# Two pairs of transformer blocks on one core: a new order at the start of the second block, the keys' rotation on GpSimd, four modulation loads moved, tables in larger steps

## The chip, the cores and the metric

The kernel runs on one core of a Trainium2 chip. A core has TensorE (PE, with its weight loads as PEld), VectorE (DVE), ScalarE (ACT), GpSimd (POOL) and the sync engine (SP), which here only issues transfers. Each engine takes its own instructions strictly in their order; semaphores tie the engines together. The metric is the device time of one execution in microseconds (us).

## The reference, cut to what matters

There are 256 tokens of width 1024. Two layers of a first block come first, and then two layers of a second block; every layer has weights of its own, all in float32.

```python
for l in range(2):                                   # first_block
    sh1, sc1, g1, sh2, sc2, g2 = split(silu(c) @ w_ada[l] + b_ada[l], 6)
    h = rms_norm(x, norm1_g[l]) * (1 + sc1) + sh1
    q, k, v, iq, ik, iw, z, xbc, dt_raw, ga, gm = split(h @ w_in[l])
    q = apply_rope(rms_norm(q), cos, sin); k = apply_rope(rms_norm(k), cos, sin)   # 16 heads of 64
    o_attn = dsa_attention(q, k, v, iq, ik, iw, 64) @ w_attn_o[l]   # each query keeps its 64 best keys
    o_ssm = ...                                      # a state space scan of z, xbc, dt
    x = x + g1 * ((sigmoid(ga) * o_attn + sigmoid(gm) * o_ssm) @ w_out[l])
    u = causal_dwconv((rms_norm(x, norm2_g[l]) * (1 + sc2) + sh2) @ w_up[l])
    x = x + g2 * ((silu(gate) * val) @ w_down[l])    # val, gate = split(u)
for l in range(2):                                   # second_block
    cq, ckv, kpe, gq, gk, gv, glr, gr, su, gates = split_in(rms_norm(x, norm1_g[l]) @ w_in[l])
    o_a = mla_mixer(cq, ckv, kpe, ...)               # 8 heads: norm, rope, softmax attention
    bc = cumsum(log_sigmoid(glr @ w_gate + b_gate) / 16)   # GLA, in chunks of 64 tokens
    o_b = gla(gq * exp(bc), gk * exp(-bc), gk * exp(b_last - bc), gv, gr)
    y = gelu(s5(su) + d * su)                        # a scan over the tokens, 512 channels
    o_c = y * sigmoid(y @ w_glu + b_glu)
    g = sigmoid(gates + gate_b).reshape(..., 3, 1024)
    merged = g[0]*(o_a @ w_br_mla) + g[1]*(o_b @ w_br_gla) + g[2]*(o_c @ w_br_s5)
    x = x + merged @ w_out[l]
    x = x + square(relu(rms_norm(x, norm2_g[l]) @ w_ff1[l])) @ w_ff2[l]
```

## The kernel before

**Weights.** All weights come from memory as one stream of pieces of 128x1024 floats, `raw`, issued on SP (L460). `make` splits each piece in two numbers of lower precision: ACT copies it into `whi` (L463), and DVE takes `raw - whi` into `wlo` (L464). There are 5 buffers of raw, 4 of whi, 3 of wlo. The activations are split alike (`hh` and `hl`, `oah` and `oal`, `yhlh` and `yhll`). A product is then three matmuls: high by high (L499), low by high (L500), high by low (L501) in `lin_t`, whose result has 128 columns of weights on the partitions and 256 tokens, and L522 to L524 in `lin_n`, whose result has the tokens on the partitions. One `lin_t` over a depth of 1024 is 24 matmuls and one piece of weights; over a depth of 512 it is 12 matmuls. Results of `lin_t` and `lin_n` lie in four PSUM buffers `pmm`; other results of PE lie in buffers `px`.

**Order.** The program is written in Python; a scheduler sets the order of each engine's instructions from the order in which the program is written, from priorities, and from the dependencies. Side work is written as generators, which `paced` advances by a few steps between two products. `tc.issue_after(x)` orders what is in its scope behind instruction x.

**First block.** The modulation (`w_ada`) comes as 48 loads a layer (`ada`, 512 KB each, in the same stream), which DVE multiplies and adds up (L718), ACT gathers (L732) and PE sums (L733). ADA_A names the columns that lie in the first stage of a layer, ADA_DOWN those of layer 1 that lie in the last stage (w_down) of layer 0. The rotation (rope, `rope_n`, L805 to L811) of q and k takes six operations of 128x512 for each of two halves of the tokens; `kr` and `qr` are the rotated keys and queries, which PE then turns (L689). The index scores and the choice of 64 keys (L986 to L989) make a `bias`, which DVE adds to the scores (L832), ACT takes exp (L838) and scales (L841), and PE turns the result (L850). `s5_prep` makes tables for the second block (L661 to L669: phases, sine and cosine) in steps beside w_up and w_down; PDN is its steps for each column of w_down.

**Second block.** `block2` makes the MLA heads' `mq`, `mk`, `mv`, then `la`, the logarithm of GLA's gate: log1p by DVE in a chain of dependent operations (`log1pexp_neg`, L676 to L683, then L1599, L1600) and the running sum `ge` (L1604, eight scans). Ten exponentials on ACT (L1606 to L1611) read it. `gv` is a `lin_n` with 512 columns, two buffers of pmm, moved out by ACT (L1617). Then comes a loop over 24 gate products n (`lin_t`, L1693 the tanh that moves each out); after n = 3 `linear_qk` is written. In each turn of the loop `paced(chain, CHAIN)` does CHAIN steps of `chains`, 35 in all: the MLA heads' norm and rope on DVE (L1650, six of L805 to L811, L1655, then four transposes L689; eight such sets), GLA, and the attention. Every third turn does a step of `s5_run`: for each quarter q of the channels L1464, L1468 to L1481, then L1489 and L1493 on PE, L1496 on ACT, a transfer to memory (L1497, on ACT's queue) and back (L1500, on SP's queue) into `yt`, and L1504. After the loop come `branch(1)` and `branch(0)` (8 products of depth 512 each), gelu (L1717) and split (L554, L555) of the S5 result, four products `s5_w_glu_2`, which give `oc` (L1725, L1726) and its split `och`, `ocl` (L551, L552), and `branch(2)`.

`slot` gives buffers of 4 KB for each partition from a pool of NSLOT; `crow` holds a row form of silu(c) for some of the ada loads.

## Time and profile before

| what | value |
|---|---|
| median of 3 runs | 2246.64 us (2245.1 to 2252.94) |
| the profiled execution | 2245.79 us |
| its span, first to last instruction | 2243.8 us |
| mean granted TensorE clock | 0.98 |
| busy share of PE, DVE, ACT, POOL | 95%, 77%, 60%, 5% |

The profile is of one execution. [...] The difference between the execution's time and its span, 2.0 us, lies around the span.

### The profile page before, as it was taken

What the parts mean: (1) busy time and instruction counts of PE and PEld (TensorE: products, weight loads), DVE (VectorE), ACT (ScalarE), POOL (GpSimd) and SP (SyncE); (2) the same over time, 40 slices, a digit from 0 to 9 for tenths busy, and PEclk for the clock granted to TensorE, in tenths of its full rate; (3) what the DMA queues carried; (4) which work ended last, traced back from release to release, by engine and by line L of the source; (5) the groups of instructions that cost most, each with busy time, mean ns of one, the idle gap of its engine ahead of it and who ended that gap; (6) DMA issues with size and microseconds to landing.
All of it is one profiled execution on the core that took longest, in us unless ns stands there. A gap on an engine that the chain in (4) does not pass through costs nothing. (4 is left out here: it accounts for less than half of the span.)

```text
span 2243.8 us, 44306 instructions
## 1 busy us (share of the span) xinstructions
PE 2140.3 (95%) x17296; PEld 2024.6 (90%) x17296; DVE 1732.6 (77%) x3349; ACT 1336.3 (60%) x2461; POOL 116.5 (5%) x122
## 2 busy tenths in 40 slices
PE   7998999999998997999989999899999997999999
PEld 6888789998997886889989998899999997999999
DVE  4888888889887888788889787677875577678753
ACT  4546866466646557775576566585664464755643
POOL 0210011000000210011000001000000010000000
PEclk9999999999999998999999999899999998999999
DMA  8755344856685653444746666444555564444553
GB/s 324 246 206 197 138 166 152 296 198 208 224 286 188 225 190 132 167 162 164 263 159 199 200 242 225 135 157 158 177 190 182 174 218 135 150 160 162 195 180 123
DMA packets 143457, 429.09 MB, mean 191 GB/s; under 512 B 34864, under 2 KB 40976, under 8 KB 143248
## 3 DMA queue, kind: packets, MB, share of 16 engines
q1 hardware_dynamic: 136496, 422.24, 55.4%
q10 hardware_dynamic: 6752, 4.02, 0.6%
q8 instruction: 136, 2.23, 0.4%
q14 instruction: 73, 0.60, 0.1%
HBM read 413.98 MB, written 12.22 MB: 190 GB/s over the span
## 5 line engine op out<-in xcount | busy, mean ns | idle before, releaser
L463 ACT ACTIVATE whi<-raw 128x1024 fp32r<-128x1024 f32 x639 | 674.8, 1059 | 592.4 <-PE pmm L500 356.1
L464 DVE TENSOR_TENSOR wlo<-raw,whi 128x1024 fp32r<-128x1024 f32 x639 | 781.8, 1225 | 295.0 <-PE pmm L501 161.8
L499 PE MATMUL pmm<-hh,whi 128*128 128x256 f32 x2432 | 698.3, 288 | 31.8 <-ACT fh L554 14.9
L501 PE MATMUL pmm<-hh,wlo 128*128 128x256 f32 x2432 | 693.0, 286 | 4.1 <-DVE wlo L464 4.1
L500 PE MATMUL pmm<-hl,whi 128*128 128x256 f32 x2432 | 694.2, 286 | 0.0
L499 PEld LDWEIGHTS pmm<-hh,whi 128*128 128x128 f32 x2432 | 470.0, 194 | 40.8 <-ACT fh L554 15.2
L501 PEld LDWEIGHTS pmm<-hh,wlo 128*128 128x128 f32 x2432 | 469.3, 194 | 9.2 <-DVE wlo L464 4.9
L500 PEld LDWEIGHTS pmm<-hl,whi 128*128 128x128 f32 x2432 | 470.5, 194 | 4.4 <-issue 3.8
L499 PE MATMUL pmm<-fh,whi 128*128 128x256 f32 x864 | 244.6, 284 | 2.1 <-ACT whi L463 2.0
L500 PE MATMUL pmm<-fl,whi 128*128 128x256 f32 x864 | 244.2, 283 | 0.0
L501 PE MATMUL pmm<-fh,wlo 128*128 128x256 f32 x864 | 243.5, 283 | 0.0
L499 PEld LDWEIGHTS pmm<-fh,whi 128*128 128x128 f32 x864 | 165.7, 192 | 2.8 <-ACT whi L463 2.5
L500 PEld LDWEIGHTS pmm<-fl,whi 128*128 128x128 f32 x864 | 165.7, 192 | 0.1
L501 PEld LDWEIGHTS pmm<-fh,wlo 128*128 128x128 f32 x864 | 165.3, 192 | 0.2
L560 POOL TENSOR_TENSOR rr<-rv,mhalf 128x2 f32<-128x2 f32 (+3 forms) x26 | 55.5, 2136 | 1173.3 <-DVE rv L565 1173.3
L523 PE MATMUL pmm<-wlo,hh 128*128 128x512 f32 x256 | 102.6, 403 | 0.0
L522 PE MATMUL pmm<-whi,hh 128*128 128x512 f32 x256 | 95.9, 403 | 1.7 <-ACT hh L548 1.5
L524 PE MATMUL pmm<-whi,hl 128*128 128x512 f32 x256 | 97.3, 398 | 0.0
L718 DVE SCALAR_TENSOR_TENSOR raw<-raw,crow 128x1024 f32<-128x1024 f32 x44 | 53.8, 1223 | 25.6 <-DMA raw<-in_ada 25.6
L499 PE MATMUL pmm<-yh,whi 128*128 128x256 f32 x256 | 71.6, 283 | 0.1
L500 PE MATMUL pmm<-yl,whi 128*128 128x256 f32 x256 | 71.5, 283 | 0.0
L501 PE MATMUL pmm<-yh,wlo 128*128 128x256 f32 x256 | 71.5, 284 | 0.0
(560 smaller groups left out, 4242.0 us busy)
## 6 DMA issues: line engine op xcount, KB each, us to landing
raw<-in_w SPq DMA_DIRECT2D x639, 512.0 KB, 4.1
raw<-in_ada SPq DMA_DIRECT2D x96, 512.0 KB, 4.5
csb<-csd SPq DMA_DIRECT2D x16, 512.0 KB, 5.7
phd<-phases SPq DMA_DIRECT2D x8, 512.0 KB, 2.9
phasel<-phd SPq DMA_DIRECT2D x8, 512.0 KB, 3.9
dpd<-dp SPq DMA_DIRECT2D x4, 512.0 KB, 3.7
gl<-gd SPq DMA_DIRECT2D x32, 64.0 KB, 3.4
bl<-in_s5b SPq DMA_DIRECT2D x4, 512.0 KB, 5.6
```

The costliest lines, as they stand in the source:

```text
L463: S.activation(hi, raw, AF.Copy)
L464: st["lo"] = V.tensor_tensor(lo, raw, hi, OP.subtract).ins
L499: PE.matmul(ps[:m, :n], wh, src.hi(kt), start=q == 0, stop=False)
L500: PE.matmul(ps[:m, :n], wh, src.lo(kt), start=False, stop=False)
L501: st["mm"] = PE.matmul(ps[:m, :n], wl, src.hi(kt), start=False, stop=q == len(kts) - 1).ins
L522: PE.matmul(ps[t][:, :n], src.hi(kt)[:, ts], w[0], start=start, stop=False)
L523: PE.matmul(ps[t][:, :n], src.hi(kt)[:, ts], w[1], start=False, stop=False)
L524: st["mm"] = PE.matmul(ps[t][:, :n], src.lo(kt)[:, ts], w[0], start=False, stop=stop).ins
L560: G.tensor_tensor(r, v, mhalf.to_broadcast([128, n]), OP.pow)
L718: V.scalar_tensor_tensor(w, w, 1.0, crow, OP.mult, OP.mult, accum_out=m)
```

## The change

The change has six parts. (1) Four modulation columns of layer 1 (20 to 23) leave layer 0's w_down and become loads of the first stage of layer 1's `block1`. (2) `crow` is a slot that is freed after its last use, and NSLOT is 21. (3) `s5_prep` does 3 steps for each column of w_down (PDN). (4) The loop over the gates does no step of `chains` at n = 0, one at n = 1 to 5, two from there on; the 35 steps end at n = 20 or later instead of n = 17. (5) The rotation of k in `block1` is on GpSimd (`G`) instead of DVE, in both layers. (6) In `block2` the ten exponentials are written behind gv and ordered behind its second eviction.

```diff
-ADA_A = (range(16, 40), range(24, 40))
+ADA_A = (range(16, 40), range(20, 40))
 ADA_X = ((), ())
 ADA_O = (range(40, 48), range(40, 48))
 ADA_UP = range(8, 16)
...
 O_FREE = 32
 GQK_AT = 4
-ADA_DOWN = range(16, 24)
+ADA_DOWN = range(16, 20)
 DOWN_TO = 110
 ADA_ROWS = {(l, c) for l, cs in ((0, (range(16, 24), range(40, 48))), (1, (range(8), range(16, 28), range(40, 48))))
...
     ps_x = ctx.enter_context(tc.tile_pool(name="psx", bufs=1, space=bass.MemoryType.PSUM))
     dram = ctx.enter_context(tc.tile_pool(name="dram", bufs=1, space=bass.MemoryType.DRAM))
-    NSLOT = 20
+    NSLOT = 21
     NFILL = 4
     PUP = 6
-    PDN = 2
+    PDN = 3
     LATE = 6
     N256 = 10
     N384 = 8
...
     NTH = 2
     NSC = 2
     LAG = 2
-    CHAIN = 2
+    CHAIN = (0,) + 5 * (1,) + 18 * (2,)
     REST_AT = 6
     PRIO = 1500
...
         V.tensor_reduce(norms[0].ss, sqs, AX.X, OP.add)
-    crow = cpool.tile([128, 1024], F32, name="crow")
+    crow = slot(name="crow").rearrange("p a b -> p (a b)")
     for q in range(2):
         pc = px()
         for j in range(4):
...
                     xr = slot(name=nm + "r").rearrange("p a b -> p (a b)")
                     x3 = xr.rearrange("p (h d) -> p h d", d=64)
                     rope_n(x3, qk[nm][t].rearrange("p (h d) -> p h d", d=64), tb[:, 0, t], tb[:, 1, t],
-                           tb[:, 2, t], tb[:, 3, t], 16, 32, V)
+                           tb[:, 2, t], tb[:, 3, t], 16, 32, G if nm == "k" else V)
                     V.tensor_tensor(x3, x3, r[:, :, None].to_broadcast([128, 16, 64]), OP.mult)
                     turn()
                     yield
...
         for q in range(8):
             V.tensor_tensor_scan(bc[:, q * 64:(q + 1) * 64], ones[:, :64], la[:, q * 64:(q + 1) * 64], 0.0,
                                  OP.mult, OP.add)
-        S.activation(eb, bc, AF.Exp)
-        ges2 = flat(slot(name="ge2"))
-        en, ke = ges2[:, 0:512], ges2[:, 512:1024]
-        S.activation(en, bc, AF.Exp, scale=-1.0)
-        for q in range(8):
-            S.activation(ke[:, q * 64:(q + 1) * 64], bc[:, q * 64:(q + 1) * 64], AF.Exp,
-                         bias=bc[:, q * 64 + 63:q * 64 + 64], scale=-1.0)
         next(steps)
         gv = flat(slot(name="gv"))
         gvN = [gv[:, t * 512:(t + 1) * 512] for t in range(2)]
         for t, p_ in enumerate(lin_n(w, h, range(8), 512)):
-            S.activation(gvN[t], p_, AF.Copy)
+            gv_out = S.activation(gvN[t], p_, AF.Copy).ins
+        ges2 = flat(slot(name="ge2"))
+        en, ke = ges2[:, 0:512], ges2[:, 512:1024]
+
+        with tc.issue_after(gv_out):
+            S.activation(eb, bc, AF.Exp)
+            S.activation(en, bc, AF.Exp, scale=-1.0)
+            for q in range(8):
+                S.activation(ke[:, q * 64:(q + 1) * 64], bc[:, q * 64:(q + 1) * 64], AF.Exp,
+                             bias=bc[:, q * 64 + 63:q * 64 + 64], scale=-1.0)
         gqk = slot(name="gqk")
         gqf, gkf = flat(gqk[:, 0:2, :]), flat(gqk[:, 2:4, :])
...
         for n in range(24):
             if n == GQK_AT:
                 linear_qk()
-            paced(chain, CHAIN)
+            paced(chain, CHAIN[n])
             if n % 3 == 2:
                 paced(steps)
             br, j = (1, 0, 2)[n // 8], n % 8
```

How this moves instructions is seen at three places. Lines from L1606 on have other numbers in the changed kernel: gv's eviction L1617 is L1610, the exponentials L1606, L1609, L1611 are L1615, L1616, L1618, and L1650 to L1726 are two lines further on.

**Place 1: ACT at the start of block2, layer 0** (`whi_17400` and `whi_17354` are the same piece of weights). Before:

```order
L463 ACTIVATE whi_17400<-raw_17398 128x1024
L1611 ACTIVATE ge2_17152<-ge_17142 128x64 x7
L1606 ACTIVATE ge_17142<-ge_17142 128x512
L1609 ACTIVATE ge2_17152<-ge_17142 128x512
L1611 ACTIVATE ge2_17152<-ge_17142 128x64
L1617 ACTIVATE gv_17202<-pmm_17203 128x512
L1617 ACTIVATE gv_17202<-pmm_17204 128x512
L1693 ACTIVATE gate_17319<-pmm_17320,gbh_17290 128x256
```

Now:

```order
L463 ACTIVATE whi_17354<-raw_17352 128x1024
L1610 ACTIVATE gv_17191<-pmm_17192 128x512
L1610 ACTIVATE gv_17191<-pmm_17193 128x512
L1618 ACTIVATE ge2_17268<-ge_17142 128x64 x7
L1615 ACTIVATE ge_17142<-ge_17142 128x512
L1616 ACTIVATE ge2_17268<-ge_17142 128x512
L1618 ACTIVATE ge2_17268<-ge_17142 128x64
L1695 ACTIVATE gate_17292<-pmm_17293,gbh_17290 128x256
L1695 ACTIVATE gate_17292<-pmm_17339,gbh_17290 128x256
L463 ACTIVATE whi_17429<-raw_17427 128x1024
```

The two evictions of gv moved from behind the exponentials to ahead of them; two gates and the next whi stand behind the exponentials. On DVE there stood four sets of L1650, L805 to L811, L1655 among the operations of log1p ahead of the scan L1604 in layer 0, and six in layer 1; now there are one and two. DVE's last rows to the scan in layer 0, now:

```order
L682 SCALAR_TENSOR_TENSOR lp_17118<-lp_17118,z2_17128 128x512
L807 TENSOR_TENSOR mq3_17326<-ru_17328,rv_17329 128x4x16
L811 TENSOR_TENSOR mq3_17326<-ru_17333,rv_17334 128x4x16
L682 SCALAR_TENSOR_TENSOR lp_17118<-lp_17118,z2_17128 128x512
L1657 TENSOR_TENSOR mq3_17326<-mq3_17326,rr_17036 128x384
L682 SCALAR_TENSOR_TENSOR lp_17118<-lp_17118,z2_17128 128x512
L683 SCALAR_TENSOR_TENSOR lp_17118<-lp_17118,z_17127 128x512
L1599 SCALAR_TENSOR_TENSOR la_17117<-la_17117,lp_17118 128x512
L1600 TENSOR_SCALAR la_17117<-la_17117 128x512
L1604 SCALAR_TENSOR_TENSOR ge_17142<-ones_79,la_17117 128x64 x8
L464 TENSOR_TENSOR wlo_17355<-raw_17352,whi_17354 128x1024
L1652 TENSOR_TENSOR mq3_17371<-mq_16965,rows_16962 128x4x64
```

One set (`mq3_17326`) stands between the L682; the next (`mq3_17371`) moved behind the scan and behind wlo_17355.

**Place 2: the last quarter of S5 in block2, layer 0** (`px_18808` is its result, `yt_18824` what comes back from memory; pmm_18995 to 19118 are branch(0), pmm_19158 to 19218 the four products of s5_w_glu_2). PE before, then now:

```order
L500 MATMUL pmm_18975<-obl_17771,whi_18876 128x256
L501 MATMUL pmm_18975<-obh_17770,wlo_18877 128x256
L1493 MATMUL px_18808<-vb_18695,dpl_18013 64x64 x8
L499 MATMUL pmm_18975<-obh_17770,whi_18876 128x256
L500 MATMUL pmm_18975<-obl_17771,whi_18876 128x256
L501 MATMUL pmm_18975<-obh_17770,wlo_18877 128x256
L499 MATMUL pmm_18975<-obh_17770,whi_18876 128x256
```

PE now:

```order
L499 MATMUL pmm_19218<-yhlh_19140,whi_19085 128x256
L500 MATMUL pmm_19218<-yhll_19141,whi_19085 128x256
L501 MATMUL pmm_19218<-yhlh_19140,wlo_19086 128x256
L1493 MATMUL px_18808<-vb_18695,dpl_17940 64x64 x8
L499 MATMUL pmm_19158<-yhlh_19140,whi_19013 128x256
L499 MATMUL pmm_19176<-yhlh_19140,whi_19049 128x256
L499 MATMUL pmm_19200<-yhlh_19140,whi_19049 128x256
L499 MATMUL pmm_19218<-yhlh_19140,whi_19085 128x256
```

L1493 of that quarter moved from within the last product of branch(1), with the eight products of branch(0) still ahead of s5_w_glu_2, to behind nine of the twelve matmuls of each of the four products of s5_w_glu_2; what follows it directly reads yhlh of the same quarter. In layer 1 it moved to the same place, from a place four products of branch(0) ahead of s5_w_glu_2. DVE at the same quarter, before:

```order
L1481 TENSOR_TENSOR vb_18695<-vb_18695,vs_18696 128x512
L464 TENSOR_TENSOR wlo_18911<-raw_18908,whi_18910 128x1024
L1702 SCALAR_TENSOR_TENSOR gate_17731<-gate_17731,pmm_18927 128x256
L1702 SCALAR_TENSOR_TENSOR gate_17731<-gate_17731,pmm_18941 128x256
...
L1705 TENSOR_TENSOR gate_17319<-gate_17319,gate_18018 128x256 x2
L1504 SCALAR_TENSOR_TENSOR uT_16686<-uT_16686,pp844_78,yt_18824 128x4x64
L464 TENSOR_TENSOR wlo_19050<-raw_19047,whi_19049 128x1024
```

DVE now:

```order
L1704 SCALAR_TENSOR_TENSOR gate_18170<-gate_18170,pmm_19118 128x256
L1707 TENSOR_TENSOR gate_17641<-gate_17641,gate_18170 128x256 x3
L1481 TENSOR_TENSOR vb_18695<-vb_18695,vs_18696 128x512
L1707 TENSOR_TENSOR gate_17641<-gate_17641,gate_18170 128x256
L1504 SCALAR_TENSOR_TENSOR uT_16686<-uT_16686,pp844_78,yt_18824 128x4x64
L555 TENSOR_TENSOR yhll_19141<-uT_16686,yhlh_19140 128x256
L464 TENSOR_TENSOR wlo_19122<-raw_19119,whi_19121 128x1024
```

Between L1481 and L1504 of that quarter there were 14 rows, four of them wlo; now there is one.

**Place 3: ACT where block1 of layer 1 begins** (`ga_8637` and `hh_8633` before are `ga_8621` and `hh_8617` now: the first activations of layer 1). Before:

```order
L948 ACT_TABLE_LOAD
L948 ACTIVATE ac_9188<-pp844_78 32x1
L667 ACT_TABLE_LOAD
L667 ACTIVATE phases_8195<-pha_8196 128x512
L668 ACTIVATE phn_8197<-pha_8196 128x512
L905 ACT_TABLE_LOAD
L905 ACTIVATE ga_8637<-upre_8642,sc_8641 128x256
L548 ACTIVATE hh_8633<-nv_8646,modb1_109 128x256
L905 ACTIVATE ga_8637<-upre_8651,sc_8650 128x256
L548 ACTIVATE hh_8633<-nv_8655,modb1_109 128x256
```

Now:

```order
L948 ACT_TABLE_LOAD
L948 ACTIVATE ac_9176<-pp844_78 32x1
L905 ACTIVATE ga_8621<-upre_8626,sc_8625 128x256
L548 ACTIVATE hh_8617<-nv_8630,modb1_109 128x256
L905 ACTIVATE ga_8621<-upre_8635,sc_8634 128x256
L548 ACTIVATE hh_8617<-nv_8639,modb1_109 128x256
```

The last phases of `s5_prep` (L667 to L669) moved ahead of this place, and with them four of the five table loads that stood here (L669's and one more of L905 stand right behind the rows shown of before).

On POOL the twelve operations L805 to L811 of `kn` and `kr` in each layer stand behind the tables of the next rotation (`tbq` of layer 1 in layer 0, `tb2q` in layer 1).

## Rows read from the trace of the kernel before

**Rows 1.** The page, busy time of each engine: us, share of the span, instructions:

```profile
PE 2140.3 (95%) x17296; PEld 2024.6 (90%) x17296; DVE 1732.6 (77%) x3349; ACT 1336.3 (60%) x2461; POOL 116.5 (5%) x122
```

**Rows 2.** Three stretches: busy us (count) by engine, PEclk, DMA, GB/s:

```profile
694.00:708.00 14.00, 6.73 (x21) 5.25 (x20) 8.12 (x20) 13.70 (x21) 0.00 (x0) 0.63 0.45 152
800.00:850.00 50.00, 45.38 (x436) 42.59 (x436) 48.63 (x111) 27.14 (x52) 5.66 (x8) 0.94 0.53 190
1399.00:1418.00 19.00, 7.71 (x36) 6.18 (x35) 13.55 (x43) 7.24 (x18) 0.12 (x1) 0.64 0.34 90
```

**Rows 3.** Timeline of PE, block2 of layer 0: start, duration, [idle <-releaser]:

```profile
1393.58 0.28 PE L501 MATMUL pmm<-hh,wlo 128*128 128x256 f32 x1
...
1398.97 0.28 PE L501 MATMUL pmm<-hh,wlo 128*128 128x256 f32 x1
1403.76 2.10 PE L689 MATMUL px<-cst,mq 128*96 128x128 f32 x8 [4.51 <-DVE mq L1655]
1407.66 1.09 PE L689 MATMUL px<-cst,mq 128*96 128x128 f32 x4 [1.79 <-DVE mq L1655]
1413.69 0.58 PE L499 MATMUL pmm<-hh,whi 128*128 128x256 f32 x1 [4.94 <-ACT gv L1617]
```

**Rows 4.** Timeline of PE, block2 of layer 1:

```profile
1857.69 2.10 PE L689 MATMUL px<-cst,mq 128*96 128x128 f32 x8 [4.78 <-DVE mq L1655]
1862.13 1.09 PE L689 MATMUL px<-cst,mq 128*96 128x128 f32 x4 [2.34 <-DVE mq L1655]
1870.60 0.58 PE L499 MATMUL pmm<-hh,whi 128*128 128x256 f32 x1 [7.38 <-ACT gv L1617]
```

**Rows 5.** Timeline of ACT at these places, layer 0, then layer 1:

```profile
1410.10 1.78 ACT L1611 ACTIVATE ge<-ge 128x64 f32<-128x64 f32 x7 [11.26 <-DVE ge L1604]
1867.01 1.78 ACT L1611 ACTIVATE ge<-ge 128x64 f32<-128x64 f32 x7 [13.12 <-DVE ge L1604]
```

**Rows 6.** Timeline of DVE in block2 of layer 0:

```profile
1401.07 0.42 DVE L1650 TENSOR_TENSOR mq<-mq,rows 128x256 f32<-128x256 f32 x1
...
1403.16 0.55 DVE L1655 TENSOR_TENSOR mq<-mq,rr 128x384 f32<-128x384 f32 x1
...
1409.77 1.56 DVE L1604 TENSOR_TENSOR_SCAN ge<-ones,la 128x64 f32<-128x64 f32 x8
```

**Rows 7.** Timeline of ACT and PE where block1 of layer 1 begins:

```profile
699.27 1.28 ACT L905 ACT_TABLE_LOAD   x1
...
700.98 0.49 ACT L548 ACTIVATE hh<-nv,modb 128x256 fp32r<-128x256 f32 x1
...
701.52 0.54 PE L913 MATMUL px<-hh,whi 128*104 128x256 f32 x1 [7.27 <-ACT hh L548]
```

**Rows 8.** Timeline of PE in the attention of block1, layer 1:

```profile
879.76 0.48 PE L850 MATMUL px<-cst,sc 128*128 128x128 f32 x1 [7.17 <-ACT sc L841]
```

**Rows 9.** Groups of DVE by form: busy us, mean ns, idle before:

```profile
L807 DVE TENSOR_TENSOR kr<-ru,rv 128x512 f32<-128x512 f32 x4 | 2.7, 679 | 0.0
```

**Rows 10.** Line L582 on POOL: duration ns min/median/max, first and last start:

```profile
L582 POOL TENSOR_TENSOR sq<-sq x24: 725/1094/2523, 307.1 to 1042.4; 128x256 f32<-128x256 f32 x24
```

**Rows 11.** Timeline of DVE before and beside the L582 that runs from 307.15:

```profile
305.50 1.21 DVE L464 TENSOR_TENSOR wlo<-raw,whi 128x1024 fp32r<-128x1024 f32 x1
...
308.37 1.43 DVE L464 TENSOR_TENSOR wlo<-raw,whi 128x1024 fp32r<-128x1024 f32 x1
```

**Rows 12.** Timeline, all engines, the last S5 quarter of layer 1:

```profile
1999.77 0.69 PE L1493 MATMUL px<-vb,dpl 128*64 128x64 f32 x16
...
2006.83 0.69 DVE L1504 SCALAR_TENSOR_TENSOR uT<-uT,pp,yt 128x256 f32<-128x256 f32 x1 [0.99 <-DMA yt<-yd]
...
2008.01 0.42 ACT L554 ACTIVATE yhlh<-uT 128x256 fp32r<-128x256 f32 x1
...
2015.30 1.22 PE L499 MATMUL pmm<-och,whi 128*128 128x256 f32 x4 [3.14 <-ACT och L551]
```

**Rows 13.** From issue to landing, transfers of L1497:

```profile
DMA to landing us min/median/max: 1.7/2.9/4.6
```

## The prediction

> **What bounds the kernel now.** The page comes first: TensorE is busy for 2140.3 of 2243.8 us, and no other engine for more than 77% [rows 1]. So a change counts by what it does to PE's idle stretches, about 100 us in all, and to the stretches in which PE works at the lower clock level. PE's waits by releaser say which idle stretches are large; the timeline of PE gives their place, and the timelines of ACT and DVE at the same microseconds say what PE waits for. The reader is to see in them that one such wait is a chain over three engines, and that a whole chain moves when one link stands elsewhere.
>
> At the start of `block2` PE ends its second gate at 1399.25 and is then idle for 4.51, 1.79 and 4.94 us [rows 3], 11.2 in all; in layer 1 for 4.78, 2.34 and 7.38, 14.5 in all [rows 4]. ACT is idle there for 11.26 and 13.12 us until the scan L1604 [rows 5], because the exponentials stand ahead of gv's eviction, and all four pmm buffers are taken until then. The release comes 3.9 us after the scan's start: 1409.77 to 1413.69 [rows 3, 6]. [...]
>
> **The start of block2, layer 0.** Three of the four rope sets leave the way to the scan. A set is L1650 (0.42), six small operations and L1655 (0.55) [rows 6]; each overlaps the next by some 0.08, and the small ones follow at 0.14: 0.34 + 0.84 + 0.47 = 1.6 us. Three are 4.9, so the scan starts at 1404.9 and gate 0's eviction, which now stands where gv's stood, releases PE 3.9 later, at 1408.8. gv is out early: ACT is free from 1410.10 less 11.26, 1398.84, and two evictions later PE has two more buffers. PE's matmuls are 0.12 us apart: 46 from 1393.58 to 1398.97 [rows 3]. Gates 2 and 3 are 48 of them, 5.8 us, and their wlo stand ahead of the scan. PE starts them 0.3 late, ends at 1405.3 and waits 3.5. So idle time falls from 11.2 to 3.8. [...] The gain is 11.2 + 3.5 - 3.8 - 3 = 7.9.
>
> **Layer 1.** Four of six sets leave, 6.5 us; the scan starts 0.32 before the exponentials' 1867.01 [rows 5], so now at 1860.2, and the release is at 1864.1. PE is free at 1857.69 less 4.78, 1852.9 [rows 4], but ACT only at 1867.01 less 13.12, 1853.9 [rows 5]; gv is out at 1854.6, gates 2 and 3 end at 1860.4, and the wait is 3.7. Idle time falls from 14.5 to 1.7 + 3.7; with the clock as above the gain is 9.6. For both I take 17, between 9 (the small waits that the deferred sets bring back eat half) and 25 (nothing is left but the first waits).
>
> **Table loads at block1 of layer 1.** PE waits 7.27 us for the first hh, which ACT starts at 700.98 [rows 7]. Four of the five table loads that stood about here are gone, of 1.28 each [rows 7], with the two long activations between. Two of these loads and those activations stand ahead of the first hh; without them it comes 3.8 us earlier. PE is at its lower level for 10.4 of 14 us there, by a mean clock of 0.63 [rows 2], and some of it goes too. I take 5, between 3.8 and 7. The extra steps of `s5_prep` lie beside w_down, where PE is full; the four ada columns that left pay for them there.
>
> **Modulation and keys.** The four ada cost four L718 of DVE in a stage before 800 in which DVE has room; what hides them is PE's products, and without that cover they cost about 5 us, one wlo's 1.2 each. `crow` as a slot costs nothing unless the pool runs dry. The keys' rotation takes 12 operations of 0.6 us (0.679 less the overlap) off DVE in each layer, 7.2 us [rows 9]. From 800 to 850 DVE is busy for 48.63 of 50 us [rows 2], so the choice of keys there, which ends in PE's wait of 7.17 at 879.76 [rows 8], comes that much earlier; I take 7 with its clock, between nothing and 10. On POOL no row has these operations. Half their columns took 0.73 to 2.52, median 1.09 [rows 10], so one is put at 2.2 (bounds 1.45 and 5.0), and twelve at 26 us a layer. The keys come some 10 us later each time, and PE turns them (L689) between other products: I take 2 us of waits, between nothing and 10. Together 5 us gained.
>
> A DVE operation beside POOL is stretched: wlo took 1.43 beside L582 and 1.21 before it [rows 11]. [...]
>
> **The tail of S5.** This speaks against the change. The chain's steps are spread to n = 20, so attention is late, and the last quarter of S5 behind it: L1493 of q = 3 now stands on PE behind three quarters of `s5_w_glu_2`, and the next matmul reads what comes out of L1493 by way of ACT, two transfers, DVE, gelu and split. Nothing is left on PE to cover it, in either layer. In layer 1 of before that way is seen under cover: L1493 ends at 2000.46, L1504 waits for the transfer until 2006.83, L554 ends at 2008.43 [rows 12]. That is 8.0 us, now an idle stretch of PE twice. Its first transfer landed in 1.7 to 4.6 us over the eight quarters, median 2.9 [rows 13], so the way is 7 to 10. Behind it the four products end within 12 matmuls, and PE waits for oc and och: 3.14 us in layer 1 today [rows 12], nothing to speak of in layer 0. So layer 0 pays 8.0 + 3.1 + 3 of clock, layer 1 8.0 + 1.5 of clock, since its wait for och stands already. Sum 23.6, between 14 (7 each, no more) and 32. DVE stands at L1504 with a wlo behind it, which is late next: it is part of the 3.1.
>
> **Sum.** The profiled time, 2245.8 (span 2243.8 and 2.0 around it; 0.8 below the median, so it is used for both): - 17 - 5 - 5 + 23.6 = 2242. That is 0.2% less, within the 0.5% (11 us) that a measurement of this kernel can tell from no change.
>
> **Rivals.** (1) The tail is cheap and the rest works: the way is 7 us and neither the second wait nor the clock come, so 14 instead of 23.6, and 2232. For it: the transfers then run with few loads beside them. Against it: PE always fell to the lower clock after waits of this length. With the wait for the choice of keys all gone too, 3 more, 2229. (2) The new order of block2 does less than it says: the two gates behind gv only move the wait to gate 4, and the sets left out return as waits at the transposes. Then that part gives 6 instead of 17, and the time is 2253. For it: the scan still gates everything; against it: 4.9 and 6.5 us are off its way for good. (3) On the other side: DVE stands behind POOL. If each of the 12 operations of a layer holds DVE for 1.45 us, twice the shortest row of L582, DVE loses 1.45 - 0.6 each, 10 us a layer; in layer 1 that is all on the path (DVE has 1.4 us of room in 50), in layer 0 half. In place of 5 gained, 15 are lost: 2262. It decides from about 1.2 us of hold, where the time passes 2257. [...]
>
> **How the numbers follow.** Forecast, 2235 to 2250: 0.38. Rival 1: 0.32. Rival 2: 0.13. Rival 3: 0.17. Faster by over 0.5% is rival 1 and a little of the forecast, 0.36; within it the rest of the forecast and rival 2, 0.47; slower rival 3, 0.17. The range from 2224 to 2259 takes in rivals 1 and 2 and half of rival 3; the forecast's own is 2235 to 2250.
>
> **What would show it.** In the new profile ACT's wait for the scan is some 6 us, gv's eviction ahead of it, and PE waits there for a gate's eviction near 3.5 us in each layer. The first hh of layer 1 waits about 3.5. PE has two new waits on yhlh of about 8 us behind L1493. The prediction is wrong if those two are under 5 or over 11, if DVE's wlo are stretched all through the keys' rotation, or if PE waits for kr for more than 5 us.

## The result, and the profile after

The changed kernel takes 2262.54 us (median of 5 executions, 2254.81 to 2264.02), the kernel before 2246.64. The ratio is 1.0063, with an interval from 1.0041 to 1.0084: slower by 0.6%, 20 us above the forecast of 2242 and just above the upper end of its range, 2259. Below, ratios are told in us as well: a thousandth of the time before is 2.25 us.

First the page of the changed kernel, busy time of each engine:

```profile
PE 2157.1 (95%) x17296; PEld 2037.5 (90%) x17296; DVE 1731.7 (77%) x3325; ACT 1329.6 (59%) x2457; POOL 153.2 (7%) x146
```

Against [rows 1], POOL has 37 us more, and DVE is as busy as before, although twelve operations of each layer left it. PE does the same 17296 instructions and is busy 17 us longer. Its idle time is 105 us instead of 103.5 and its mean granted clock 0.977 instead of 0.980. In both traces the granted clock is 1.00 or 0.50 and nothing else; it is 0.50 for 89 us of the kernel before, in which PE is busy for 55, and for 106 us of the changed one, in which PE is busy for 80. So PE waits about as long as before, but more of its work ran at 0.50, the lower clock. What that costs is seen in the changed kernel: matmuls of 128x256 that follow one another start 0.213 us apart at 0.50 (1566.38 to 1568.72) and 0.120 us apart at 1.00 (1571.11 to 1571.71). An estimate from these two figures (1 - 0.120/0.213), used below: 0.44 of PE's busy time at 0.50 is lost. Then PE's waits by releaser in the changed kernel, in us in total, their number, and the longest:

```profile
PE pmm L499 <- ACT yhlh L554: 13.8, 2, 7.1
...
PE pmm L499 <- ACT gate L1695: 7.5, 2, 4.0
...
PE px L913 <- ACT hh L548: 5.8, 2, 3.4
...
PE pmm L499 <- ACT och L551: 4.9, 2, 2.6
...
PE px L571 <- POOL sq L582: 2.0, 1, 2.0
...
PE px L689 <- DVE kr L1021: 1.6, 2, 1.1
```

The waits on `mq` and nearly all of those on `gv` [rows 3, 4] are gone; a wait on a gate's eviction stands in their place, as forecast. The first `hh` of layer 1 waits 3.40 instead of 7.27 [rows 7]. New are the two waits on `yhlh`, and small ones on the rotated keys (`kr`) and on `sq`, which GpSimd makes. The start of `block2` in layer 0 of the changed kernel, DVE, ACT and PE, as start, duration, and idle time before:

```profile
1405.36 1.57 DVE L1604 TENSOR_TENSOR_SCAN ge<-ones,la 128x64 f32<-128x64 f32 x8
```

```profile
1398.94 1.07 ACT L1610 ACTIVATE gv<-pmm 128x512 f32<-128x512 f32 x2
1405.69 1.78 ACT L1618 ACTIVATE ge<-ge 128x64 f32<-128x64 f32 x7 [5.69 <-DVE ge L1604]
...
1408.65 0.81 ACT L1695 ACTIVATE gate<-pmm,gbh 128x256 f32<-128x256 f32 x2
```

```profile
1409.15 0.58 PE L499 MATMUL pmm<-hh,whi 128*128 128x256 f32 x1 [3.58 <-ACT gate L1695]
```

`gv` leaves as soon as it is ready (1398.94), ACT then waits 5.69 for the scan, and PE waits 3.58 in place of 11.2. All of it lies within half a microsecond of what was forecast. The tail of S5 in layer 1 of the changed kernel, by the timelines of PE, DVE and ACT (ACTq is ACT's transfer queue):

```profile
2020.32 0.69 PE L1493 MATMUL px<-vb,dpl 128*64 128x64 f32 x16 [1.44 <-DVE vb L1481]
...
2027.75 1.22 PE L499 MATMUL pmm<-yhlh,whi 128*128 128x256 f32 x4 [6.74 <-ACT yhlh L554]
...
2033.26 1.22 PE L499 MATMUL pmm<-och,whi 128*128 128x256 f32 x4 [2.57 <-ACT och L551]
```

```profile
2026.13 0.67 DVE L1504 SCALAR_TENSOR_TENSOR uT<-uT,pp,yt 128x256 f32<-128x256 f32 x1 [5.87 <-DMA yt<-yd]
```

```profile
2021.47 0.33 ACTq L1497 DMA_DIRECT2D yd<-yj  x1
2021.83 1.28 ACT L1719 ACT_TABLE_LOAD   x1 [0.39 <-ACT yj L1496]
2026.84 0.42 ACT L1719 ACTIVATE uT<-uT 128x256 f32<-128x256 f32 x1 [3.73 <-DVE uT L1504]
2027.29 0.42 ACT L554 ACTIVATE yhlh<-uT 128x256 fp32r<-128x256 f32 x1
```

From L1493 the way goes over ACT, two transfers (issued at 2021.47, through by 2026.13), DVE, gelu and the split, and PE stands through it. In [rows 12] the same way of 8 us lay under matmuls. The granted clock there and at three other places is seen in five stretches of the changed kernel (columns as in [rows 2]):

```profile
694.00:708.00 14.00, 10.39 (x82) 9.79 (x81) 10.15 (x18) 10.69 (x22) 0.70 (x1) 1.00 0.71 214
800.00:850.00 50.00, 44.89 (x437) 40.69 (x439) 47.90 (x107) 21.04 (x42) 23.58 (x20) 0.93 0.48 169
1405.00:1424.00 19.00, 15.14 (x103) 14.68 (x103) 15.82 (x46) 12.43 (x24) 0.37 (x1) 0.82 0.60 164
2018.00:2046.00 28.00, 17.24 (x130) 16.61 (x129) 15.88 (x33) 11.59 (x21) 0.00 (x0) 0.76 0.30 104
1554.00:1580.00 26.00, 17.78 (x122) 17.49 (x123) 15.67 (x31) 11.88 (x21) 0.00 (x0) 0.74 0.34 112
```

and, for the last two, the same work in the kernel before:

```profile
1996.00:2024.00 28.00, 24.86 (x206) 24.46 (x205) 20.83 (x41) 12.35 (x20) 0.00 (x0) 0.94 0.45 149
1546.00:1572.00 26.00, 24.25 (x196) 23.52 (x196) 21.77 (x45) 12.66 (x22) 0.00 (x0) 1.00 0.48 166
```

Where block1 of layer 1 begins (694 to 708) the granted clock rose from 0.63 [rows 2], with 0.50 from 697.37 to 707.61, to 1.00, and at the start of `block2` from 0.64 to 0.82. At the two tails it fell, from 1.00 to 0.74 in layer 0 and from 0.94 to 0.76 in layer 1, and in stretches of the same length PE is busy for 6.5 and 7.6 us less. From 800 to 850, beside the choice of keys, DVE is busy for 47.90 us where it was 48.63, although the keys' rotation has left it.

Where the time went can be read off by PE's own instructions: both kernels have 17296, so the start of its n-th instruction in one profile less that in the other says how far the one is behind at that point. For some n, with the time before in the first row (us, from the two traces, later ones included for use below):

```
n                 1000  3000  5250  6000  8500 10500 10900 11400 12100 14000 14300 14800 15700
before, time       146   400   675   809  1126  1376  1446  1503  1588  1817  1881  1935  2048
changed           +4.5  +9.7 +10.0  +4.6  -0.2  +0.2  -7.6  -4.4  +9.8  +9.8  -0.1  +6.4 +18.4
old CHAIN (e3)    +3.8 +12.5 +12.1  +7.9  +5.0  +5.9  +0.7  +1.6  +1.0  +1.0  -6.4  -5.6  -3.8
steep CHAIN (e15) +2.1  +3.2  +0.9  -3.0  -7.6  -7.1 -14.9 -10.1  +2.5  +2.5  -7.3  +2.4  +3.3
ada, slot (e16)   +0.4  -2.8  +0.3  -4.2  +2.9  +3.1  +3.2  +4.1  +4.0  +4.0  +3.7  +3.6  +5.0
S5 early (e1)     +3.3  +3.5  +3.9  -2.0  -5.0  -4.2 -11.9 -13.9 -10.2 -10.2 -23.2 -16.1 -14.2
e1, k DVE (e12)   -0.2  -0.6  +2.1  -3.5  -5.5  -4.2 -13.8 -14.5 -10.8 -10.8 -21.9 -21.4 -22.5
```

In the changed kernel the two starts of `block2` (10500 to 10900 and 14000 to 14300) give 7.8 and 9.9, the GLA stages behind them (to 11400 and 14800) take back 3.2 and 6.5, and the tails (to 12100 and 15700) cost 14.2 and 12.0. In the GLA stage of layer 1 PE waits four times for `gst`, 1.9 us in all, and is granted 0.89 from 1915 to 1945, where the kernel before has 1.00 from 1910 to 1940. Around n = 6000 PE's order differs a good deal between the kernels, so that column is good to a few us only. (e12 is e1 with the keys of layer 0 back on DVE.) In the first block 10.0 is lost in layer 0 (n = 5250) and 10.2 given back by n = 8500. That pair must be read with care: single profiles of nearly the same order in layer 0 lie 8 us and more apart (last section).

### The profile page after: what moved, and what is told of

Its sections match the earlier page's. It is cut to its first block, busy times and chain, and to the rows that moved or that the text cites. A ratio compares the mean times of both kernels' runs of the same rounds, so it can differ in the third digit from the quotient of the medians.

```text
span 2262.2 us, 44296 instructions
## 1 busy us (share of the span) xinstructions
PE 2157.1 (95%) x17296; PEld 2037.5 (90%) x17296; DVE 1731.7 (77%) x3325; ACT 1329.6 (59%) x2457; POOL 153.2 (7%) x146
```

## The experiments

Sixteen kernels ran. "Changed" is the kernel of the diff; each ratio is to the kernel before on the same chip.

| run | against | edit | median us | ratio (95% interval) |
|---|---|---|---|---|
| the change | | | 2262.54 | 1.0063 (1.0041 to 1.0084) |
| e1_s5_early | changed | S5 steps earlier | 2231.69 | 0.9937 (0.9916 to 0.9958) |
| e2_krope_dve | changed | keys on DVE | 2258.5 | 1.0045 (1.0024 to 1.0067) |
| e3_chain_old | changed | CHAIN 2 all through | 2233.29 | 0.9944 (0.9924 to 0.9964) |
| e4_krope_only | before | keys on GpSimd | 2257.89 | 1.0049 (1.0025 to 1.0073) |
| e5_chain_old_kdve | changed | e2 and e3 | 2232.75 | 0.9909 (0.9875 to 0.9944) |
| e6_s5_early_kdve | changed | e1 and e2 | 2236.38 | 0.9942 (0.9923 to 0.9962) |
| e7_exps_only | before | exponentials behind gv | 2230.51 | 0.9932 (0.9904 to 0.996) |
| e8_k_pool_layer1 | changed | e3, GpSimd in layer 1 only | 2228.12 | 0.9903 (0.9879 to 0.9926) |
| e9_idle_tensor | before | 24 idle GpSimd products | 2262.97 | 1.0075 (1.0046 to 1.0105) |
| e10_idle_memset | before | 24 idle GpSimd fills | 2246.42 | 0.9998 (0.9982 to 1.0014) |
| e11_pdn3_only | before | PDN = 3 | 2246.33 | 0.9998 (0.9983 to 1.0013) |
| e12_best_parts | changed | e1, GpSimd in layer 1 only | 2226.83 | 0.9907 (0.988 to 0.9933) |
| e13_after_k_layer1 | changed | GpSimd in layer 1 only | 2260.05 | 1.0063 (1.0043 to 1.0082) |
| e14_after_k_layer0 | changed | GpSimd in layer 0 only | 2265.54 | 1.0084 (1.0066 to 1.0102) |
| e15_chain_steep | changed | CHAIN 3 from n = 6 | 2252.0 | 1.0031 (1.0017 to 1.0044) |
| e16_ada_slot_only | before | four ada, crow a slot | 2246.26 | 1.0 (0.9986 to 1.0014) |

### Is it the late tail?

e1 leaves CHAIN as changed and advances the S5 steps by itself, so that L1493 has some 200 matmuls of other products behind it, more than before the change:

```diff
-            if n % 3 == 2:
+            if n in (1, 4, 6, 9, 11, 14, 16, 19):
                 paced(steps)
```

> The changed kernel, but the eight S5 steps in the loop over the gates stand at n = 1, 4, 6, 9, 11, 14, 16, 19 instead of every third turn, so that L1493 of the last quarter has 201 and 214 matmuls of other products behind it on PE before yhlh of that quarter is read, where the changed kernel has none. Theory 1 (the uncovered way through two transfers is what block2 lost): both waits on yhlh, 7.06 and 6.74 us, go, with them the waits on och and the lower clock; 2262 falls by 16 to 24, to 2238 to 2246. Rival (the spread chain costs by itself, because GLA and attention come later and beside fewer products): the waits only move, and the time stays above 2255.

0.9937: 28 us off the changed kernel, faster than the kernel before and below the range of theory 1. No wait on `yhlh` is left. The late tail thus costs more than the change lost in all, and it is dearer than the 23.6 of the forecast.

e3 undoes CHAIN alone:

```diff
-    CHAIN = (0,) + 5 * (1,) + 18 * (2,)
+    CHAIN = 24 * (2,)
```

> The changed kernel with two steps of the chain at each of the 24 gates, as before; the exponentials stay behind gv's eviction. Theory 1 (CHAIN moved both the scan and the tail): the tail's waits on yhlh go (L1493 has 117 and 89 matmuls behind it again), but four and six rope sets stand ahead of the scan again, so that the wait for a gate's eviction grows from 3.6 and 4.0 to about 8 and 10 us; together 2262 falls by 8 to 14, to 2248 to 2254. Rival (the exponentials' place makes the start, CHAIN only the tail): the wait stays near 4 and the time falls to about 2243.

0.9944, so 27 us off, more than either theory gave. The theory that the rope sets put off make the gain at the start fell: with all sets back ahead of the scan, PE waits 4.51 and 1.66 on `mq` in layer 0, but the third wait, on `gv` [rows 3], is gone, and nothing waits on a gate. e7 shows that one part of the diff does this by itself, the exponentials' place:

> The kernel before with one edit, the ten exponentials written behind gv and ordered behind its second eviction; two steps of the chain at every gate. Theory 1 (this edit alone makes the gain at the start of block2): the waits on gv, 4.94 and 7.38, go, the waits on mq of 6.3 and 7.1 stay, and some lower clock goes; 2247 becomes 2229 to 2236. Rival (the rope sets ahead of the scan must go too, as the prediction had it): the wait moves to a gate's eviction and the time stays at 2241 or more.

Its edit is the hunk of `block2` that moves the exponentials behind `gv`, made in the kernel before. 0.9932, 15 us faster; the first two waits on `mq` stay, the third is gone. So the gain at the start belongs to the exponentials, and what the spread CHAIN adds at the start it loses again. The pairs in which neither kernel has the long waits on `yhlh` (CHAIN spread and the S5 steps early, against CHAIN of before) say the same: e1 against e3 -2 us, e12 against e8 +1, e6 against e5 +7.

e15 keeps the start of the spread and ends the chain at n = 15 instead of 20:

```diff
-    CHAIN = (0,) + 5 * (1,) + 18 * (2,)
+    CHAIN = (0,) + 5 * (1,) + 18 * (3,)
```

> The changed kernel, but CHAIN goes to 3 steps a product from n = 6 on instead of 2, so the start of block2 is as in the change and the chain ends at n = 15 instead of 20. The last L1493 of layer 1 then stands where it stood before the change, that of layer 0 38 matmuls ahead of its place in the change. Theory 1 (the late end of the chain is what costs): 2235 to 2243, yhlh waits under 2 us in layer 1 and about 4 in layer 0, waits at the start as in the change (3.5 and 4). Theory 2 (the sets put off cost as well, since they come back beside GLA): 2245 to 2252, with waits in the GLA stage as in the change or larger.

1.0031, 7 us off the changed kernel and at the upper end of what theory 2 gave. Its waits in the two tails (timeline of PE, layer 0, then the only one left in layer 1):

```profile
1552.63 1.23 PE L499 MATMUL pmm<-yhlh,whi 128*128 128x256 f32 x4 [5.89 <-ACT yhlh L554]
1557.92 1.22 PE L499 MATMUL pmm<-och,whi 128*128 128x256 f32 x4 [2.36 <-ACT och L551]
...
2018.40 0.74 PE L499 MATMUL pmm<-och,whi 128*128 128x256 f32 x4 [3.14 <-ACT och L551]
```

In layer 1, where L1493 is back at its place of before, the tail costs 0.9 (+2.4 to +3.3 in the table above), so theory 1 holds there; in layer 0 the 38 matmuls shorten the wait by 1.2 only, to 5.89 where theory 1 had about 4, and the tail still costs 12.6. The GLA stage takes back 4.8 and 9.7, all that the start gave in layer 1. So both theories hold in part: where the tail is cured its cost is gone, and the sets put off come back all the same.

### The keys on GpSimd

e2 puts them back on DVE in the changed kernel; e4 moves them alone, in the kernel before.

```diff
-                           tb[:, 2, t], tb[:, 3, t], 16, 32, G if nm == "k" else V)
+                           tb[:, 2, t], tb[:, 3, t], 16, 32, V)
```

> The changed kernel with the keys' rotation back on DVE. Theory 1 (GpSimd's twelve operations hold DVE and bring about the 10 us that block1 of layer 0 lost): block1 of layer 0 ends 8 to 11 us earlier, block1 of layer 1 loses the 3 us that it gained; 2262 falls to about 2255. Rival (layer 0 lost them to the order of side work and loads, from the slot pool and the moved ada columns, not to GpSimd): layer 0 stays within 3 us of the changed kernel, and the time is 2262 to 2268.

> The kernel before with one edit, the keys' rotation on GpSimd. Theory 1 (GpSimd costs layer 0 about 10 us and gives layer 1 some 8): 2246 becomes 2244 to 2252, with the loss in layer 0 to be seen between 130 and 480 us. Rival (DVE is freed of 7 us a layer and nothing is held): layer 0 unchanged, the wait of 7.17 at the choice of keys in layer 1 gone, 2234 to 2240.

e2 gains 4 us (1.0045, an interval that overlaps the change's), between its two theories; e4 loses 11 (1.0049), more than either of its theories gave. The wait of 7.17 [rows 8] is gone in e4, but 3.61 on `kr` at 165.75 and three of about 2 near 837, 885 and 888 have come. What happens beside GpSimd is seen in layer 0 of the changed kernel, timelines of POOL and of DVE:

```profile
140.41 2.27 POOL L805 TENSOR_TENSOR ru<-kn,tbk 128x512 f32<-128x512 f32 x1
143.12 2.10 POOL L806 TENSOR_TENSOR rv<-kn,tbk 128x512 f32<-128x512 f32 x1 [0.45 <-DVE bias L980]
145.30 2.13 POOL L807 TENSOR_TENSOR kr<-ru,rv 128x512 f32<-128x512 f32 x1
147.51 1.25 POOL L809 TENSOR_TENSOR ru<-kn,tbk 128x512 f32<-128x512 f32 x1
```

```profile
144.01 2.29 DVE L464 TENSOR_TENSOR wlo<-raw,whi 128x1024 fp32r<-128x1024 f32 x1
146.23 0.42 DVE L986 MAX8 m<-bias 128x8 f32<-128x256 f32 x1
...
148.07 1.77 DVE L464 TENSOR_TENSOR wlo<-raw,whi 128x1024 fp32r<-128x1024 f32 x1
...
155.06 1.97 DVE L1021 TENSOR_TENSOR kr<-kr,rr 128x1024 f32<-128x1024 f32 x1
...
157.34 1.92 DVE L464 TENSOR_TENSOR wlo<-raw,whi 128x1024 fp32r<-128x1024 f32 x1
```

L806 ends at 145.22. The wlo that began beside it ends at 146.30, 1.08 later, about the 1.21 that one took undisturbed [rows 11]; L807, which began beside that wlo, ends 1.13 after it, at 147.43. The wlo at 148.07 ends at 149.84, again 1.08 after L809. In these rows they take turns whole, each standing until the other is through; L986, with one input, takes 0.42, the mean of its eight of this shape in the kernel before. Of the five wlo beside the rotation these two and the one at 157.34 took 1.77 to 2.29 us, the other two 1.34 and 1.22. Whether it is the reading of operands from SBUF was tried in e9 and e10: idle work on GpSimd in the kernel before, after each rotation of k.

```diff
+                    if nm == "k":
+                        for _ in range(6):
+                            G.tensor_tensor(qk["k"][t][:, :512], qk["k"][t][:, :512], qk["k"][t][:, 512:], OP.mult)
```

> The kernel before, with the keys' rotation on DVE as it was, and twelve further GpSimd operations in each layer, whose results nothing reads: tensor by tensor multiplications of 128x512 that read two operands from SBUF, placed behind each half of the keys' rotation, on its dead input. Theory 1 (what GpSimd's rotation costs in layer 0 is that its operations hold DVE): DVE's wlo and other two-operand operations beside them take 1.5 to 2.3 us instead of 1.2, and the time rises by 4 to 12 us, to 2251 to 2259. Rival (the cost is that the keys come late, or only the order of the side work): no DVE operation is stretched by more than 0.2 us and the time is 2244 to 2250.

> As the run with idle multiplications, but the twelve further GpSimd operations of a layer are fills of 128x1024 with zero, which read nothing. Theory 1 (only a GpSimd operation that reads holds DVE): about as long on GpSimd, DVE's operations beside them unstretched, the time 2244 to 2250. Rival (any GpSimd operation beside DVE costs): stretched as beside the multiplications, and 2251 or more.

e10 has `G.memset(qk["k"][t], 0.0)` in the loop instead. The results of the idle work are not read. DVE's groups from 130 to 175 us (busy us, mean ns | idle before) for e9:

```profile
L464 DVE TENSOR_TENSOR wlo<-raw,whi 128x1024 fp32r<-128x1024 f32 x10 | 14.0, 1395 | 1.2 <-ACT whi L463 1.2
...
L811 DVE TENSOR_TENSOR kr<-ru,rv 128x512 f32<-128x512 f32 x2 | 2.3, 1170 | 0.0
```

and for e10, with POOL's from 130 to 260:

```profile
L464 DVE TENSOR_TENSOR wlo<-raw,whi 128x1024 fp32r<-128x1024 f32 x11 | 13.7, 1241 | 1.4 <-ACT whi L463 1.4
...
L811 DVE TENSOR_TENSOR kr<-ru,rv 128x512 f32<-128x512 f32 x2 | 1.4, 680 | 0.0
```

```profile
L1023 POOL MEMSET kn<- 128x1024 f32 x12 | 11.5, 958 | 16.8 <-DVE rv L810 16.3
```

Twelve products a layer that nobody waits for cost 17 us in all (1.0075, more than theory 1 gave), twelve fills of 0.96 us nothing (0.9998), and only beside the products do DVE's operations stretch: L811 from 0.68 to 1.17, the wlo from 1.24 to 1.40 in the mean. The busy time of each engine over the whole execution, e9, then e10:

```profile
PE 2140.6 (95%) x17296; PEld 2025.0 (90%) x17296; DVE 1752.5 (78%) x3349; ACT 1336.1 (59%) x2461; POOL 156.9 (7%) x146
PE 2136.4 (95%) x17296; PEld 2022.8 (90%) x17296; DVE 1732.6 (77%) x3349; ACT 1335.3 (60%) x2461; POOL 139.4 (6%) x146
```

Against [rows 1] DVE, with the same 3349 operations, is busy for 20 us more beside the products and for nothing more beside the fills. PE's instructions stand in the same order in both runs and in the kernel before, so a new order is not the cause. Products, which read two operands from SBUF, stretched DVE's operations, and fills, which read nothing, did not; what makes the one engine stand for the other is not shown.

Six more runs split the two layers. e8 is e3, e12 is e1 and e13 the changed kernel, all with GpSimd in layer 1 only; e14 is the changed kernel with `l == 0` in that place; e5 and e6 are e3 and e1 with the keys on DVE.

```diff
-                           tb[:, 2, t], tb[:, 3, t], 16, 32, G if nm == "k" else V)
+                           tb[:, 2, t], tb[:, 3, t], 16, 32, G if nm == "k" and l == 1 else V)
```

> The changed kernel with two parts undone: two steps of the chain at every gate, and the keys' rotation on DVE; exponentials behind gv, ada columns, slots and PDN stay. Theory 1 (GpSimd's rotation costs 4 to 10 us whatever the rest is): 2233 with the chain alone undone becomes 2223 to 2229. Rival (what GpSimd costs in layer 0 it gives back in layer 1): 2230 to 2236.

> The changed kernel with the S5 steps early and the keys' rotation on DVE; the chain stays spread. Theory 1: as for the chain of before, 4 to 10 us less than with the early steps alone (2232), so 2222 to 2228. Rival: within 3 us of 2232.

> The changed kernel with two steps of the chain at every gate and the keys' rotation on GpSimd in layer 1 alone. Theory 1 (in layer 0 GpSimd holds DVE ahead of a stage that waits for wlo, in layer 1 it frees the choice of keys): 3 to 6 us below the kernel with both on DVE. Rival (GpSimd costs in both layers): 2 to 6 us above it.

> The changed kernel with the S5 steps early and the keys' rotation on GpSimd in layer 1 alone; exponentials behind gv, spread chain, ada columns, slots and PDN 3 stay. Theory 1 (the spread chain is worth some 2 us a layer at the start and costs some 5 a layer in GLA, once the tail is covered): 2226 to 2233, not below the same kernel with two steps at every gate (2228). Rival (the spread chain was good but for the tail): 2218 to 2225.

> The changed kernel, but GpSimd turns the keys in layer 1 only; layer 0's are back on VectorE. [...] Theory 2 (the place of the rotation is worth nothing, and the few us between these versions are scatter): 2258 to 2263.

> The changed kernel, but GpSimd turns the keys in layer 0 only. Theory 1: dearer than both all on GpSimd (2262.5) and all on VectorE (2258.5), 2264 to 2270, with the stretched L464 of VectorE beside the rotation in layer 0 and a wait of 5 to 7 us in layer 1's choice of keys. Theory 2: 2258 to 2263.

e13, at 2260.05, is what theory 2 gave, with a wait of 4.29 on `kr` in layer 1; e14, at 2265.54, what theory 1 gave, though the choice of keys waits 3.08 and not 5 to 7. e5 came out as its rival, e6 (2236.38) as neither of its theories; e8 is below e5 as theory 1 had it, by 4.6 us in the medians but by 1 in the ratios, and e12 as its theory 1. By ratios: GpSimd in layer 0 costs 0 (changed against e13), 9 (e14 against e2), 9 (e3 against e8) and 7 us (e1 against e12), 6 in the mean. In layer 1 it costs 4 us (e13 against e2) or saves 5 (changed against e14), 1 (e8 against e5) and 8 (e12 against e6), a saving of 2.5 in the mean. Each ratio has an interval of 4 to 8 us on either side, and the difference of two a wider one. The layer 0 cost is seen in three pairs of four, the layer 1 saving is not told from nothing. e12 is the fastest of all, 0.9907, level with e8. PE in its two tails, the same work as in the stretches shown of the changed kernel:

```profile
1535.00:1561.00 26.00, 25.19 (x207) 24.82 (x207) 22.03 (x46) 12.70 (x21) 0.00 (x0) 1.00 0.48 166
1978.00:2006.00 28.00, 27.79 (x231) 27.59 (x230) 23.09 (x45) 15.41 (x23) 0.00 (x0) 1.00 0.50 169
```

207 and 231 matmuls in the time in which the changed kernel did 122 and 130, at a granted clock of 1.00.

### Tables, modulation, slots

e11 is PDN alone, e16 the ada columns and `crow` alone, both in the kernel before.

```diff
-    PDN = 2
+    PDN = 3
```

```diff
-ADA_A = (range(16, 40), range(24, 40))
+ADA_A = (range(16, 40), range(20, 40))
...
-ADA_DOWN = range(16, 24)
+ADA_DOWN = range(16, 20)
...
-    NSLOT = 20
+    NSLOT = 21
...
-    crow = cpool.tile([128, 1024], F32, name="crow")
+    crow = slot(name="crow").rearrange("p a b -> p (a b)")
```

> The kernel before with one edit, three steps of s5_prep for each column of w_down. Theory 1 (the table loads at the start of layer 1 are what this edit moves): the first wait on hh there falls from 7.27 to 3.4, block1 of layer 1 begins 4 to 6 us earlier, and the time is 2241 to 2244. Rival (what it gains there it loses in w_down): 2246 to 2250.

> The kernel before with the four modulation columns moved to layer 1's first stage and crow as one of 21 slots, nothing else. Theory 1 (these parts are worth nothing in the median): 2244 to 2249. Theory 2 (it is they that move the table loads): the first hh of layer 1 waits 3.4 instead of 7.27, and the time is 2240 to 2244.

PDN moves nothing: the `hh` wait stays 7.27 and the ratio is 0.9998. The theory that it moves the table loads fell. e16 moves them, as theory 2 said, and its ratio is 1.0000, as theory 1 said. Its timeline of PE shows both ends:

```profile
697.64 0.54 PE L913 MATMUL px<-hh,whi 128*104 128x256 f32 x1 [3.40 <-ACT hh L548]
...
876.65 0.47 PE L850 MATMUL px<-cst,sc 128*128 128x128 f32 x1 [5.36 <-ACT sc L841]
```

The `hh` wait fell by 3.9, and the wait for the choice of keys from 7.17 [rows 8] to 5.36, but from 809 to 1126 us this kernel loses some 7 (-4.2 to +2.9 in the table above). What costs them is not shown. In the trace of e16 DVE adds up the four ada between 724 and 764 us, ahead of the choice of keys, which begins at 803; no run moves them without the slot.

## Why the prediction was wrong, point by point

**The tail of S5** was right in mechanism and place. The waits on `yhlh` are 7.06 and 6.74 where 8.0 was forecast, those on `och` 2.36 and 2.57 where it was 3.1, and in layer 1 PE also waits 1.44 for `vb`, which the forecast did not have. No run shows the 3 and the 1.5 of clock that the sum takes. What the runs show in their place comes close: from 1555.3 to 1568.9 and from 2022.9 to 2036.5 PE was granted 0.50, with 6.68 and 6.17 us of work. By the estimate of 0.44 that is 2.9 lost in layer 0 and 2.7 in layer 1; the kernel before already lost some 1.3 of these (0.50 from 2014.92 to 2018.33, with 3.03 us of work), which leaves 1.4. The tails cost 14.2 and 12.0 in the profile, 26.2 against 23.6; beside these waits and the clock some 5 us are left that the rows do not place. By the timed pairs that differ only in the S5 steps it is 28 (changed, e1), 35 (e13, e12) and 23 (e2, e6): 29 in the mean.

**The start of block2** came as forecast where it lies: 17.7 in the profile against 17, with waits of 3.58 and 3.95 against 3.5 and 3.7. No run shows the 3.5 of clock before and the 3 after that its sum takes. In their place the kernel before was granted 0.50 from 1403.93 to 1417.59 and from 1857.90 to 1874.97, with 6.89 and 7.28 us of work, and the changed one from 1408.55 to 1415.38 and from 1872.76 to 1879.59, with 5.95 and 5.44: by the same estimate 3.0 and 3.2 lost before, 2.6 and 2.4 after. What it was credited to was wrong: "4.9 and 6.5 us are off its way for good" does not hold. The GLA stages took back 9.7 of the 17.7, and e7 gains 15 us (interval 9 to 22) without moving a set. Rival 2 was right in that half, and wrong that the two gates only move the wait.

**The steps that failed** are the two gains of 5. "Table loads at block1 of layer 1 ... I take 5" is right about the wait, which fell by 3.9, and wrong about the time: with the four ada and the slot alone, e16 measured 1.0000, so as much was lost behind it. The next part had put the ada at nothing ("what hides them is PE's products"); whether it is they that cost it stays open. "Modulation and keys ... Together 5 us gained" took a 2.2 us operation on POOL and 7 us off the choice of keys. The operations' time was about right (the twelve of layer 0 ran from 140.41 to 163.21, 22.8 us where 26 was put), but the engine it was taken from got no relief: DVE stood behind POOL. 24 operations of 0.6 us, 14 us, left DVE, and its busy time fell by 0.9 us in the changed kernel and by 1.7 in e4 (1730.9). One of the signs that the prediction had named came with it, the stretched wlo, three of five in layer 0. Rival 3 has this mechanism with too large a hold: it puts 1.45 us on each operation moved and asks for 1.2 to decide, and DVE's busy time gives 0.5 to 0.6 (12.7 to 13.5 us over 24 operations), which eats the gain and no more. Yet GpSimd in place of DVE costs 4 (changed, e2), 8 (e3, e5), -1 (e1, e6) and 11 us (e4, before), 5 in the mean; new waits of PE such as the 3.61 on `kr` are part of that.

**The sum** by the runs: exponentials -15, table loads with ada 0, PDN 0, keys +5, tail +29 make +19; the change measured +14 (1.0063, interval 9 to 19). Against the forecast the keys miss by 10, the tables by 5, the tail by 5 and the start by 2, all to the same side. That rival 3's time, 2262, came out is luck: its one cause is less than half of it. Rival 1, the cheap tail, is refuted: the second wait and the clock of 0.50 are there in both layers. The reason that the prediction gave against it held too: the five waits of 7.06 to 7.80 in the kernel before all ended at a granted 0.50.

What stays open: why the keys cost 11 us alone in the kernel before and 4 in the changed one, which the intervals allow to be the same; and why the spread CHAIN costs the GLA stage of layer 1 7 us in e1 and 0.5 in e12, which is equal but for layer 0's keys. The trace of e1 shows at least where:

```profile
1898.46 0.61 PE L689 MATMUL px<-cst,mq 128*96 128x128 f32 x4 [3.76 <-DVE mq L1657]
```

A set that was put off comes back there as a wait at the transposes, as rival 2 said, and PE is granted 0.86 from 1895 to 1920; e12 has no such wait in that stage and is granted 1.00 from 1890 to 1915.

## What to carry to other kernels

When steps of side work are put off to clear one wait, follow the last of them to the end of the loop: a result that went through memory and back took 8.0 us here [rows 12] and left PE waiting 6.74 and 7.06 where no other work lay behind it, and an earlier issue of that one chain (e1) was worth 28 us, twice what the whole change lost. Before work goes to GpSimd from a loaded VectorE, look at what stands beside it there: three of the five wlo, which read two operands, took 1.77 to 2.29 us beside the rotation where one took 1.21 alone [rows 11], and idle work on GpSimd priced this in one run (17 us in e9). A wait that gets shorter is no gain until the work that left it is found where it went.

## What was unexpected of the hardware

The stretches at the lower granted clock differ between executions of one order. In layer 0 of the first block e7, e11 and e10 have PE's order of the kernel before, but for one exchanged pair at most, and yet their profiles stand 8.2 and 5.7 us behind it and 6.4 ahead of it at 675 us. In e7 a part of that is seen: from 220 to 245 us PE is granted 0.73, where the kernel before has 1.00 from 219 to 244. Over 23 executions the kernel before ranges from 2240.57 to 2252.26. A stage of layer 0 can thus not be priced from one profile to better than some 8 us. From n = 5250 to 10500 the same three move by no more than 2.2 us, so later stages are safer, and waits mostly repeat to the tenth (the `och` wait of 3.14 stands in [rows 12] and again in e15 and e16). After a like wait the granted clock differed too: around the 3.95 for a gate in layer 1 the changed kernel is granted 0.82 (1870 to 1889), around the 3.11 for the same gate e1 has 1.00 (1840 to 1859).

And 24 idle operations on an engine that is busy 5% of the time cost the kernel 17 us, while 24 fills on it cost nothing.
